# Head pairs of the value product side by side, wider transposes of maxima, another bank for denominators and another band entry, in a two-layer encoder

## The chip, the cores and the metric

The kernel runs on one core of a Trainium2 chip. The metric is the device time of one execution in microseconds (us). Five engines work beside each other, each through its own queue of instructions in a fixed order: TensorE (PE; its loads of stationary operands are listed apart, as PEld), VectorE (DVE), ScalarE (ACT), GpSimd (POOL) and SyncE (SP), which starts the DMA transfers. PE writes its results into PSUM, which has eight banks of 128 partitions x 512 float32; the other engines read them from there.

## The reference

An encoder trunk of two layers over 1024 tokens of width 1024, float32 throughout. Each layer adds a mixer and then a SwiGLU feed-forward part to the stream, each behind an RMS norm:

```python
for layer in range(DEPTH):                      # DEPTH = 2
    u = rms_norm(h, g_mix[layer])
    if layer % 2 == 0:
        h = h + mla_stick_breaking_mixer(u, ...)   # 8 + 8 heads of 64
    else:
        h = h + chunk_band_mixer(u, ...)           # 16 heads of 64
    u = rms_norm(h, g_ffn[layer])
    h = h + swiglu(u, w_gate[layer], w_up[layer], w_down[layer])
return rms_norm(h, g_final)
```

The mixer of the first layer has eight heads of latent attention (MLA: queries and keys through low-rank projections, a rotary part, a softmax under a block-causal mask) and eight heads of stick-breaking attention (strictly causal, no softmax). That of the second layer is a band attention: each chunk of 64 tokens sees itself and the eight chunks ahead of it, with a learned bias by clipped relative distance, and a softmax. What the change touches is the end of each attention: `p @ v` for every head, the softmax's denominators (the sum of the exponentials), and the row maxima that are taken off ahead of the exponential.

## The kernel before, in words

**Tiles.** Everything is held transposed, features on partitions and tokens along the free axis, in tiles of 128 x 512; the 1024 tokens are two halves of 512 (`hf` 0 and 1). A product in full precision is three passes over split operands (`mm3`, lines 286 to 291: high x high, low x high, high x low); the value product, the denominators and the transposes of maxima take plain float32, for which the trace shows two records per instruction.

**Stages,** by the trace: the norm and the stick-breaking heads from 0 to 400 us, MLA with the output projection to 640, the first feed-forward part to 1326, the band's entry to 1384, six band pairs of heads to 1726 (57 us each), the last two and the output projection to 1840, the second feed-forward part to the end.

**Attention.** Heads go in pairs, one of them on partitions 0 to 63 and the other on 64 to 127. For a pair and a half of the queries, `soft_step` goes over the key tiles `j` of 128 keys: scores for both heads into a two-bank tile "z", exponentials on ACT into a tile "a" (2 x 512), their running sum on POOL ("b", line 1085; DVE in the last pairs), and, some steps later, `weighted`, the value product. It adds, for each head `e`, 64 x 128 values times 128 keys x up to 512 queries into half of the partitions of one output bank "o": two instructions, for e = 0 and e = 1, that write columns `cs` of the partitions `rh`. Later key tiles have fewer columns (512, 384, 256, 128). When the last tile is in, `soft_finish` sums the exponentials over the keys with a product with ones, again one instruction per head (line 1101) into the first bank of a "z" tile; ACT makes the reciprocal from Ln and Exp (lines 1103, 1104), DVE improves it with one Newton step (1105, 1106) and multiplies the output with it (1107).

**Maxima.** Ahead of a pair's half, all its scores are computed once for their row maxima: `mla_max` (line 1062, maxima on DVE in line 1064), `band_max` (line 1188, maxima on DVE in line 1191). `neg_max_rows` collects the maxima in one of two 128 x 2 x 32 tiles `maxes` (line 1044), turns 36 columns of it with a product with the identity into a "z" tile (line 1046), and DVE multiplies rows 0 to 3 and 32 to 35 into the queries as additional rows (line 1048), which the score products (lines 1133 to 1135 in MLA, 1214 and 1215 in the band) then read.

**PSUM.** Three kinds of tile share the eight banks: "mm" (two of one bank, for projections), "z" (two of two banks, for scores, maxima, denominators) and "o" (two of one bank, for outputs and statistics of the norms). A tile is handed out again when its last reader is done.

**What sets the order.** In the mixers the code only gives the dependences and an order of writing, with the attention's steps and the projections of the next pair woven together (`weave`); a list scheduler with a cost model then sets the order on each engine. In the feed-forward parts instructions stay in the order of the program.

**Band entry.** `to_mixer1` takes each finished tile of the first feed-forward part, and with the last tile of a half `close` computes the statistics of the norm (line 322 on PE, line 352 for those by column). `mixer1` then computes the values of the first two head pairs for both halves (`vgen(0, [0, 1])`), the first pair's queries and keys (`band_project`; for this pair DVE casts the weights' high parts) and its maxima.

## Time and profile before

| what | value |
|---|---|
| median of 3 runs | 2552.98 us (2551.01 to 2554.29) |
| profiled execution | 2553.58 us |
| its span in the trace | 2551.9 us |
| mean granted clock of PE | 0.995 |
| chain that ended last, by engine | PE 74%, DVE 8%, DMA 1%, ACT 1% |

The busy time of an engine is given for the whole span and for stretches of it; a stretch in which PE is nearly always busy is shortened only by less work for PE or by closing the gaps that are there. In a timeline, the start of an instruction and the start of the next one on the same engine say more than its duration, since products overlap: full-width three-pass products of 512 columns follow each other every 0.23 us, though each lasts 0.39. "x4" are four records of the same form that follow each other directly. Behind an instruction stands in brackets for how long its engine had been idle, and what ended that.

### The profile page before, as it was taken

To read this page: it belongs to the slowest core of one execution; us is meant where nothing else is said; L and a number is where in the kernel's file an instruction comes from. 1 tells how busy PE (TensorE), PEld (TensorE's weight loads), DVE (VectorE), ACT (ScalarE), POOL (GpSimd) and SP (SyncE) were. 2 spreads that over 40 slices of the span, in tenths; PEclk is the share of its full clock that TensorE was granted. 3 is DMA by queue.
4 is the path that set the end of the run, shared out by engine and by line. 5 is a ranking of instruction groups with operands and counts; after the bars stand their busy time and mean duration, and the time that the engine had idled before them with its cause. 6 is when DMAs were issued, how large, how long until landed. Compare 5 with 4: busy or idle time off the path is not lost.

```text
span 2551.9 us, 33625 instructions
## 1 busy us (share of the span) xinstructions
PE 2478.1 (97%) x11710; PEld 1938.4 (76%) x11710; DVE 1858.1 (73%) x3072; ACT 1152.1 (45%) x1996; POOL 493.8 (19%) x475
## 2 busy tenths in 40 slices
PE   9999989999999999999999999999999999999997
PEld 7776766557778888888888777776777888888886
DVE  7988796565886666677766777777788676667775
ACT  5777565344454434433353443334445443443324
POOL 0333335652000000000031334345200000000004
PEclk9999999999999999999999999999999999999998
DMA  5222102125434334476652222223633433447661
GB/s 155 54 65 64 41 26 60 54 84 165 153 124 149 120 128 145 149 259 211 227 167 69 79 87 75 75 93 98 190 128 128 148 130 118 145 156 261 217 208 71
DMA packets 182250, 323.91 MB, mean 127 GB/s; under 512 B 21312, under 2 KB 37568, under 8 KB 182080
## 3 DMA queue, kind: packets, MB, share of 16 engines
q1 hardware_dynamic: 182080, 321.76, 38.0%
q8 instruction: 93, 1.52, 0.2%
q14 instruction: 77, 0.63, 0.1%
HBM read 222.58 MB, written 84.41 MB: 120 GB/s over the span
## 4 chain that ended last, share of the span: by engine, by line
PE 74%; DVE 8%; DMA 1%; ACT 1%; issue 1%; POOL 0%; DVEq 0%; SPq 0%; ACTq 0%; POOLq 0%
PE z L76 25%; PE mm L76 13%; PE o L76 7%; PE mm L289 6%; PE mm L290 6%; PE mm L291 6%; PE o L844 4%; DVE u L76 2%; PE z L1214 1%; PE z L1188 1%; PE z L1215 1%; PE z L1133 1%; DVE u L312 1%; PE z L1101 1%; PE z L1134 1%
## 5 line engine op out<-in xcount | busy, mean ns | idle before, releaser
L76 PE MATMUL z<-u,wh 128*128 128x512 f32 x976 | 302.3, 390 | 6.5 <-DVE u L76 6.5
L76 PE MATMUL z<-u,vh 128*128 128x512 f32 x976 | 301.8, 390 | 2.8 <-DVE u L76 2.8
L289 PE MATMUL mm<-u,wh 128*128 128x512 f32 x720 | 287.8, 400 | 3.5 <-DVE f L1003 1.4
L290 PE MATMUL mm<-u,wh 128*128 128x512 f32 x720 | 283.8, 394 | 0.0
L291 PE MATMUL mm<-u,wl 128*128 128x512 f32 x720 | 282.4, 393 | 0.0
L257 POOL TENSOR_TENSOR wl<-wr,wh 128x512 fp32r<-128x512 f32 (+2 forms) x95 | 122.0, 1289 | 803.3 <-ACT wh L252 736.0
L76 PE MATMUL mm<-u,wh 128*128 128x512 f32 x720 | 223.4, 392 | 4.6 <-ACT wh L76 4.6
L76 PEld LDWEIGHTS z<-u,wh 128*128 128x128 f32 x976 | 183.2, 188 | 47.5 <-DVE u L76 9.5
L76 PEld LDWEIGHTS z<-u,vh 128*128 128x128 f32 x976 | 182.9, 188 | 43.1 <-ACT u L76 4.4
L76 PE MATMUL z<-u,wl 128*128 128x512 f32 x488 | 190.0, 389 | 1.4 <-DVE wl L76 1.4
L76 PE MATMUL z<-u,vl 128*128 128x512 f32 x488 | 189.9, 389 | 0.0
L289 PEld LDWEIGHTS mm<-u,wh 128*128 128x128 f32 x720 | 135.4, 188 | 54.7 <-issue 27.6
L76 PEld LDWEIGHTS mm<-u,wh 128*128 128x128 f32 x720 | 134.7, 188 | 35.6 <-ACT wh L76 6.9
L290 PEld LDWEIGHTS mm<-u,wh 128*128 128x128 f32 x720 | 135.5, 188 | 27.2 <-issue 3.2
L291 PEld LDWEIGHTS mm<-u,wl 128*128 128x128 f32 x720 | 135.3, 188 | 27.3 <-issue 0.9
L844 PE MATMUL o<-a,u 128*64 128x512 f32 (+3 forms) x768 | 154.6, 474 | 0.0
L76 PE MATMUL mm<-u,vh 128*128 128x512 f32 x496 | 152.7, 389 | 0.0
L76 PE MATMUL mm<-u,wl 128*128 128x512 f32 x360 | 140.8, 391 | 0.8 <-DVE wl L76 0.5
L257 POOL TENSOR_TENSOR u<-wr,u 128x512 fp32r<-128x512 f32 x8 | 10.9, 1374 | 669.5 <-ACT u L252 669.5
L1085 POOL TENSOR_TENSOR b<-b,a 128x512 f32<-128x512 f32 (+3 forms) x80 | 110.1, 1377 | 125.8 <-ACT a L1217 104.1
L1216 DVE TENSOR_TENSOR a<-z,bias 128x1024 f32<-128x1024 f32 (+3 forms) x96 | 78.2, 823 | 76.9 <-PE z L1215 71.0
L76 ACT CAST vh<-vr 128x512 fp32r<-128x512 f32 (+1 forms) x166 | 96.1, 579 | 82.5 <-DVE vr L76 31.5
(244 smaller groups left out, 5859.4 us busy)
## 6 DMA issues: line engine op xcount, KB each, us to landing
u<-f_t SPq DMA_DIRECT2D x144, 256.0 KB, 5.0
vr<-in_w_up SPq DMA_DIRECT2D x88, 256.0 KB, 4.4
wr<-in_w_gate SPq DMA_DIRECT2D x88, 256.0 KB, 3.7
f_t<-x SPq DMA_DIRECT2D x72, 256.0 KB, 2.0
wr<-in_w_out SPq DMA_DIRECT2D x64, 256.0 KB, 3.1
f_t<-e SPq DMA_DIRECT2D x54, 256.0 KB, 3.6
ld<-f SPq DMA_DIRECT2D x54, 256.0 KB, 5.1
u<-u SPq DMA_DIRECT2D x96, 128.0 KB, 2.2
```

What stands on the lines that cost most here:

```text
L76: return lambda *a, **k: self.tc.keep_in_program_order(f(*a, **k))
L257: self.eng(eng).tensor_tensor(lo, src, hi.bitcast(F32), ALU.subtract)
L289: mm(out, wh, xh, start=first, stop=False, skip_group_check=onto)
L290: mm(out, wh, xl, start=False, stop=False, skip_group_check=onto)
L291: mm(out, wl, xh, start=False, stop=last, skip_group_check=onto)
L312: self.eng(eng).tensor_tensor(acc, acc, sq, ALU.add)
L844: self.nc.tensor.matmul(o[rh, cs], vt[j // 4][:, j % 4, rh], w[:, e, cs], start=first, stop=last)
L1085: self.eng("dve" if dest[2] else "pool").tensor_tensor(st["esum"][:, :, cs], old[:, :, cs], ex[:, :, cs], ALU.add)
L1101: nc.tensor.matmul(den[64 * e:64 * e + 64, :], self.ones[:, 0:64], esum[:, e, :], start=True, stop=True)
L1133: mm(z[:, e, cs], kth[0:kr, bs], qh[0:kr, cs], start=True, stop=False)
L1134: mm(z[:, e, cs], kth[0:96, bs], ql[0:96, cs], start=False, stop=False)
L1216: nc.vector.tensor_tensor(ex[:, :, cs], z[:, :, cs], tk[:, :, xs], ALU.add)
```

## The change

There are four parts. First, `weighted` writes head 1's instruction with the highest priority and with the condition that it is issued right behind head 0's (`joined`, which keeps the last such instruction in `self.joint`); the two instructions of a denominator are tied in the same way. Second, `maxes` has 2 x 64 columns instead of 2 x 32, all 128 columns are turned, and the rows read are 0 to 3 and 64 to 67. Third, the denominators go into an "o" bank. Fourth, the band's entry runs in another order: values of half 0, then the closing of half 1 (moved there from the end of the feed-forward part), the first pair's projection, and then the values of half 1, for which the value weights are loaded and split a second time; the first pair's high parts are cast by ACT instead of DVE.

```diff
@@ -29,6 +29,7 @@
 LOADS = 4
 AHEAD = 2
 LAG = 2
+TOP = 100000
 
 TOGETHER = 4
 G_MIX0, G_FFN0, G_MIX1, G_FFN1, G_FIN, G_CQ, G_CKV, G_N = 0, 8, 16, 24, 32, 40, 43, 45
@@ -228,7 +229,7 @@
         self.tri, self.carry_ones = self.masks[:, 0:P], self.masks[:, P:2 * P]
         self.zeros = self.masks[:, 2 * P:3 * P]
 
-        self.maxes = [cp.tile([P, 2, 32], F32, name=f"maxes{i}") for i in range(2)]
+        self.maxes = [cp.tile([P, 2, 64], F32, name=f"maxes{i}") for i in range(2)]
         for m in self.maxes:
             nc.vector.memset(m, 0.0)
         self.negblk = small[0:4, 16:20]
@@ -837,11 +838,22 @@
                 v, q = vts[g][hf][:, r, :], ps[:, (b - b0) * ncol + g * P:][:, :P]
                 self.nc.scalar.activation(v, q, AF.Identity, scale=s.rc[hf][:, r:r + 1])
 
-    def weighted(self, o, vt, j, w, cs, first, last):
-
-        for e in range(2):
+    def joined(self, make, *args):
+
+        with self.tc.high_priority(offset=TOP), self.tc.issue_after(self.joint.ins):
+            self.joint = make(*args)
+
+    def weighted(self, o, vt, j, w, cs, first, last, join=False):
+
+        def head(e):
             rh = slice(64 * e, 64 * e + 64)
-            self.nc.tensor.matmul(o[rh, cs], vt[j // 4][:, j % 4, rh], w[:, e, cs], start=first, stop=last)
+            return self.nc.tensor.matmul(o[rh, cs], vt[j // 4][:, j % 4, rh], w[:, e, cs], start=first, stop=last)
+
+        if join:
+            self.joined(head, 0)
+        else:
+            self.joint = head(0)
+        self.joined(head, 1)
 
 
 
@@ -1043,10 +1055,10 @@
         m = self.maxes[0]
         nc.vector.reduce_max(m[:, :, 0:4], m2[:, :, :, :nh], axis=AX.X)
         mt = self.banks()
-        nc.tensor.matmul(mt[0:36, 0, 0:P], m.rearrange("p a b -> p (a b)")[:, 0:36], self.ident, start=True, stop=True)
+        nc.tensor.matmul(mt[:, 0, 0:P], m.rearrange("p a b -> p (a b)"), self.ident, start=True, stop=True)
         for e in range(2):
             nc.vector.tensor_tensor(dsts[e].rearrange("p (a b) -> p a b", a=4),
-                                    mt[32 * e:32 * e + 4, 0, None, 0:P].to_broadcast([4, 4, P]),
+                                    mt[64 * e:64 * e + 4, 0, None, 0:P].to_broadcast([4, 4, P]),
                                     self.negblk[:, :, None].to_broadcast([4, 4, P]), ALU.mult)
 
     def mla_max(self, hf, proj):
@@ -1096,9 +1108,13 @@
 
     def soft_finish(self, o, esum, row, k, keep):
         nc = self.nc
-        den = self.banks()[:, 0, :]
-        for e in range(2):
-            nc.tensor.matmul(den[64 * e:64 * e + 64, :], self.ones[:, 0:64], esum[:, e, :], start=True, stop=True)
+        den = self.out_bank()
+
+        def total(e):
+            return nc.tensor.matmul(den[64 * e:64 * e + 64, :], self.ones[:, 0:64], esum[:, e, :], start=True, stop=True)
+
+        self.joint = total(0)
+        self.joined(total, 1)
         r, ot = self.tmp("f"), self.tmp("f")
         nc.scalar.activation(r, den, AF.Ln)
         nc.scalar.activation(r, r, AF.Exp, scale=-1.0)
@@ -1144,7 +1160,7 @@
 
         nc, a = self.nc, self.a
         for i in range(2):
-            w = self.weight(a["w_qk1"][2 * p + i], eng_hi="dve", eng_lo="dve" if p == 0 else "pool")
+            w = self.weight(a["w_qk1"][2 * p + i], eng_hi="act" if p == 0 else "dve", eng_lo="dve" if p == 0 else "pool")
             for hf in hfs:
                 ps = self.bank()
                 yield from self.dense(ps, w, s.u[hf], range(KD))
@@ -1316,10 +1332,12 @@
             vts = [[] for _ in range(8)]
             vgen = lambda g, hf: self.values([a["w_v1"][2 * g], a["w_v1"][2 * g + 1]], u, 4, KD, 1,
                                              vts[2 * g:2 * g + 2], hf)
-            self.now(vgen(0, [0, 1]))
+            self.now(vgen(0, [0]))
+            self.close(u, 1, columns=True)
             new = lambda: ([[], []], [[], []])
             proj = new()
             self.now(self.band_project(0, u, proj))
+            self.now(vgen(0, [1]))
             tq, tk = self.band_bias(0, "bias_q"), self.band_bias(0, "bias_k")
             self.now(self.band_max(0, proj, tq))
             for p in range(8):
@@ -1363,7 +1381,7 @@
             h = s.h[hf][m]
             self.feed(nxt, hf, h, G_MIX1 + m)
             nc.sync.dma_start(h1_d[hf][m], h)
-            if m == KD - 1:
+            if m == KD - 1 and hf == 0:
                 self.close(nxt, hf, columns=True)
 
         with self.phase("ffn0", FFN_TEMPS):
```

By engine, PE keeps its number of instructions, DVE keeps its own (four subtractions more and four casts less), ACT has 8 more, SP has 4 more (transfers of 256 KB). The order on PE is the same up to the middle of the first MLA pair, and in the feed-forward parts. Three places show what moves. A row gives the line, the operation, output<-inputs and the output's shape; a number behind a name tells buffers apart, and "x2" is both heads, one behind the other. Lines 844, 1046, 1062, 1101 and 1133 to 1135 are lines 850, 1058, 1074, 1114 and 1149 to 1151 after the change, and 289 to 291 are 290 to 292.

PE before, in the first MLA pair (o816: its output bank, z: scores, a: exponentials of one key tile, u: values, queries and keys):

```order
L844 MATMUL o816_4094<-a799_4014,u698_3592 64x512
L1133 MATMUL z818_4098<-u658_3450,u733_3777 128x512
L1134 MATMUL z818_4098<-u659_3451,u733_3777 128x512
L1135 MATMUL z818_4098<-u658_3450,u734_3778 128x512
L1133 MATMUL z818_4098<-u685_3552,u736_3785 128x512
L1134 MATMUL z818_4098<-u686_3553,u736_3785 128x512
L1135 MATMUL z818_4098<-u685_3552,u737_3786 128x512
L1062 MATMUL z820_4108<-u754_3846,u785_3961 128x128
L1062 MATMUL z820_4108<-u757_3854,u805_4047 128x128
L844 MATMUL o816_4094<-a799_4014,u698_3592 64x512
L844 MATMUL o816_4094<-a802_4033,u698_3592 64x512
L1133 MATMUL z822_4115<-u658_3450,u733_3777 128x384
```

PE after, at the same place:

```order
L1149 MATMUL z818_4098<-u658_3450,u733_3777 128x512
L1150 MATMUL z818_4098<-u659_3451,u733_3777 128x512
L1151 MATMUL z818_4098<-u658_3450,u734_3778 128x512
L1149 MATMUL z818_4098<-u685_3552,u736_3785 128x512
L1150 MATMUL z818_4098<-u686_3553,u736_3785 128x512
L1151 MATMUL z818_4098<-u685_3552,u737_3786 128x512
L1074 MATMUL z820_4108<-u754_3846,u785_3961 128x128
L1074 MATMUL z820_4108<-u757_3854,u805_4047 128x128
L850 MATMUL o816_4094<-a799_4014,u698_3592 64x512 x2
L1149 MATMUL z822_4115<-u658_3450,u733_3777 128x384
L1150 MATMUL z822_4115<-u659_3451,u733_3777 128x384
```

Before, head 1 of tile a799 stands eight instructions behind its head 0 and beside head 0 of tile a802; after, both heads of a799 stand together, and a802 follows later.

PE before, in a later MLA pair, from the last scores for the maxima (z954) to the transpose (z955) and the first scores that need it (z958; mm: a projection):

```order
L1062 MATMUL z954_4665<-u852_4243,u882_4366 128x512
L1062 MATMUL z954_4665<-u855_4251,u903_4458 128x512
L289 MATMUL mm1002_4865<-u681_3538,wh1000_4861 128x512
L290 MATMUL mm1002_4865<-u682_3539,wh1000_4861 128x512
L291 MATMUL mm1002_4865<-u681_3538,wl1001_4862 128x512
L1046 MATMUL z955_4673<-ident_153,maxes0_161 36x128
L1133 MATMUL z958_4681<-u882_4366,u840_4198 128x512
```

PE after, from the same scores on:

```order
L1074 MATMUL z954_4665<-u852_4243,u882_4366 128x512
L1074 MATMUL z954_4665<-u855_4251,u903_4458 128x512
L290 MATMUL mm965_4704<-u596_3176,wh963_4700 128x512
L291 MATMUL mm965_4704<-u597_3177,wh963_4700 128x512
L850 MATMUL o956_4677<-a920_4536,u700_3596 64x512 x2
L292 MATMUL mm965_4704<-u596_3176,wl964_4701 128x512
L850 MATMUL o956_4677<-a929_4569,u700_3596 64x384 x2
L290 MATMUL mm965_4704<-u601_3198,wh963_4700 128x512
L291 MATMUL mm965_4704<-u602_3199,wh963_4700 128x512
L292 MATMUL mm965_4704<-u601_3198,wl964_4701 128x512
L850 MATMUL o956_4677<-a944_4620,u700_3596 64x256 x2
L850 MATMUL o956_4677<-a951_4651,u700_3596 64x128 x2
```

and then:

```order
L1114 MATMUL o974_4750<-b931_4578,ones_151 64x512 x2
L1058 MATMUL z955_4673<-ident_153,maxes0_161 128x128
L290 MATMUL mm1002_4865<-u674_3516,wh1000_4861 128x512
L291 MATMUL mm1002_4865<-u675_3517,wh1000_4861 128x512
L292 MATMUL mm1002_4865<-u674_3516,wl1001_4862 128x512
L1149 MATMUL z958_4681<-u882_4366,u840_4198 128x512
```

Before, one triple of a projection stands between the scores z954 and the transpose; after, two triples' worth of projections, four value products of o956 and the denominator o974, and one triple stands between the transpose and z958.

PE before, at a denominator of another MLA pair (z1031) and the first value product of the next half (o1048):

```order
L291 MATMUL mm1030_4957<-u625_3304,wl1029_4954 128x512
L1101 MATMUL z1031_4963<-b968_4722,ones_151 64x512 x2
L1133 MATMUL z1035_4975<-u960_4693,u934_4589 128x128
L1134 MATMUL z1035_4975<-u961_4694,u934_4589 128x128
L1135 MATMUL z1035_4975<-u960_4693,u935_4590 128x128
L1133 MATMUL z1035_4975<-u972_4743,u937_4597 128x128
L1134 MATMUL z1035_4975<-u973_4744,u937_4597 128x128
L1135 MATMUL z1035_4975<-u972_4743,u938_4598 128x128
L844 MATMUL o1048_5011<-a994_4844,u701_3598 64x512 x2
```

PE after, at the same denominator, which is now in an output bank (o1031):

```order
L1114 MATMUL o1031_4963<-b968_4722,ones_151 64x512 x2
L1149 MATMUL z1035_4975<-u960_4693,u934_4589 128x128
L1150 MATMUL z1035_4975<-u961_4694,u934_4589 128x128
L1151 MATMUL z1035_4975<-u960_4693,u935_4590 128x128
L1149 MATMUL z1035_4975<-u972_4743,u937_4597 128x128
L1150 MATMUL z1035_4975<-u973_4744,u937_4597 128x128
L1151 MATMUL z1035_4975<-u972_4743,u938_4598 128x128
L290 MATMUL mm1030_4957<-u625_3304,wh1028_4953 128x512
L291 MATMUL mm1030_4957<-u626_3305,wh1028_4953 128x512
L292 MATMUL mm1030_4957<-u625_3304,wl1029_4954 128x512
L290 MATMUL mm1030_4957<-u630_3326,wh1028_4953 128x512
```

and then:

```order
L291 MATMUL mm1030_4957<-u631_3327,wh1028_4953 128x512
L292 MATMUL mm1030_4957<-u630_3326,wl1029_4954 128x512
L1074 MATMUL z1058_5047<-u934_4589,u1025_4946 128x512
L850 MATMUL o1048_5011<-a994_4844,u701_3598 64x512 x2
L850 MATMUL o1048_5011<-a1013_4900,u701_3598 64x384 x2
```

Before, the six scores stand between the two; after, two triples of a projection and one instruction of the maxima's scores more, and the denominator and o1048 take turns in the output banks.

## Rows read from the trace of the kernel before

**Rows 1.** The page, part 1: busy us, share of the span, instructions, by engine

```profile
PE 2478.1 (97%) x11710; PEld 1938.4 (76%) x11710; DVE 1858.1 (73%) x3072; ACT 1152.1 (45%) x1996; POOL 493.8 (19%) x475
```

**Rows 2.** Stretches: us, then PE, PEld, DVE, ACT, POOL busy (instructions), granted clock, DMA

```profile
400.00:640.00 240.00, 232.62 (x1021) 148.72 (x1021) 146.79 (x194) 99.46 (x156) 125.25 (x91) 0.99 0.32 97
...
1326.00:1384.00 58.00, 58.00 (x349) 50.90 (x348) 28.42 (x56) 16.48 (x35) 7.13 (x8) 1.00 0.20 61
1384.00:1726.00 342.00, 333.60 (x1934) 259.40 (x1935) 253.81 (x558) 140.27 (x246) 135.51 (x134) 1.00 0.26 82
```

**Rows 3.** Timeline of PE, a pair alone: start us, us, instruction, count, [idle before]

```profile
198.12 0.39 PE L291 MATMUL mm<-u,wl 128*128 128x512 f32 x1
198.44 1.08 PE L844 MATMUL o<-a,u 128*64 128x512 f32 x4
199.45 0.50 PE L289 MATMUL mm<-u,wh 128*128 128x512 f32 x1
199.79 0.39 PE L290 MATMUL mm<-u,wh 128*128 128x512 f32 x1
```

**Rows 4.** The same, one head alone

```profile
421.98 1.07 PE L844 MATMUL o<-a,u 128*64 128x512 f32 x2
422.98 0.50 PE L289 MATMUL mm<-u,wh 128*128 128x512 f32 x1
```

**Rows 5.** The same, a pair and one head more

```profile
440.65 1.93 PE L844 MATMUL o<-a,u 128*64 128x512 f32 x6
442.51 0.50 PE L1133 MATMUL z<-u,u 104*128 104x512 f32 x1
```

**Rows 6.** One line's instructions, lines 844 and 1046: count, ns, first and last start, forms

```profile
L844 PE MATMUL o<-a,u x768: 272/486/644, 72.0 to 1836.1; 128*64 128x512 f32 x72, 128*64 128x256 f32 x41, 128*64 128x384 f32 x40, 128*64 128x128 f32 x39
L1046 PE MATMUL z<-ident,maxes x48: 271/272/300, 411.7 to 1796.3; 128*36 128x128 f32 x48
```

**Rows 7.** Timeline of PE around a transpose of maxima with 36 columns

```profile
1455.69 0.39 PE L290 MATMUL mm<-u,wh 128*128 128x512 f32 x1
1456.01 0.41 PE L1046 MATMUL z<-ident,maxes 128*36 128x128 f32 x2
...
1456.69 0.39 PE L291 MATMUL mm<-u,wl 128*128 128x512 f32 x1
```

**Rows 8.** The same around a full-width product in plain float32, two passes

```profile
347.81 1.02 PE L322 MATMUL o<-u,ones 128*128 128x512 f32 x2
...
348.90 0.40 PE L290 MATMUL mm<-u,wh 128*128 128x512 f32 x1
```

**Rows 9.** Waits of PE, 400 to 640 us: us in total, times, longest

```profile
PE z L1046 <- DVE maxes L1044: 3.8, 2, 2.0
PE z L1133 <- DVE u L1048: 1.0, 1, 1.0
```

**Rows 10.** Timeline of PE around the longest of these waits

```profile
521.70 0.62 PE L1062 MATMUL z<-u,u 104*128 104x512 f32 x2
...
525.05 0.38 PE L1046 MATMUL z<-ident,maxes 128*36 128x128 f32 x2 [2.04 <-DVE maxes L1044]
```

**Rows 11.** Windows after it, columns as in the stretches

```profile
528.00:530.00 2.00, 2.00 (x6) 1.52 (x6) 0.50 (x1) 1.92 (x3) 1.28 (x1) 0.50 0.31 83
530.00:532.00 2.00, 2.00 (x8) 1.62 (x7) 0.69 (x1) 1.03 (x3) 0.00 (x0) 0.76 0.02 8
```

**Rows 12.** Timeline of all engines, a typical denominator, lines 1101 to 1106

```profile
438.03 1.08 PE L1101 MATMUL z<-b,ones 128*64 128x512 f32 x4
...
441.19 0.69 DVE L1106 SCALAR_TENSOR_TENSOR f<-z,f 128x512 f32<-128x512 f32 x1
```

**Rows 13.** Timelines of PE and DVE, the slowest denominator

```profile
1746.63 1.08 PE L1101 MATMUL z<-b,ones 128*64 128x512 f32 x4
...
1753.24 0.68 DVE L1106 SCALAR_TENSOR_TENSOR f<-z,f 128x512 f32<-128x512 f32 x1
```

**Rows 14.** Waits of PE, 1384 to 1726 us

```profile
PE z L1214 <- DVE a L1216: 7.3, 6, 1.2
```

## The prediction

> **What bounds the kernel now.** I read the shares of the span by engine first. TensorE (PE) is busy for 2478.1 of 2551.9 us, 97%; VectorE (DVE) follows with 1858.1, 73% [rows 1]. So the span is a sum of PE instructions with few gaps, and two things can shorten it: PE work that becomes cheaper, and gaps that close. Next I read the busy time stage by stage [rows 2]. In the attention of the first layer (400 to 640 us) PE is busy for 232.62 of 240 us, in the band pairs (1384 to 1726) for 333.60 of 342, and at the band's entry (1326 to 1384) for all 58.00. DVE has 146.79 of 240 and 253.81 of 342: room, but in the band not much. Then the gaps: in the first layer's attention the largest are waits for the row maxima and for what is made of them [rows 9], in the band six equal ones of 1.2 us behind the scores' bias add [rows 14]. The profiled execution took 2553.58 us, 0.60 above the median of 2552.98, so a sum made against it is lowered by 0.6 at the end.
>
> **Part 1, the second head's product behind the first's.** One head's product is two float32 passes that use half of the array's columns. What a pass costs follows from three places in the timeline. Two heads side by side, 512 columns each, start at 198.44 and the next instruction at 199.45: 1.01 us for four passes [rows 3]. One head alone goes from 421.98 to 422.98: 1.00 us for two passes [rows 4]. So the second head beside the first costs nothing. A pair and one head more, also 512 wide, take 440.65 to 442.51, 1.86 us [rows 5]. The head that has no neighbour costs 0.85 us. What is left of the 1.01 is a price per run of such products, 0.16, and the full-width instructions at both edges add to it: the first start comes 0.32 after its predecessor and the second neighbour follows 0.34 after the first, where the pace of such instructions is 0.23 [rows 3]. That is 0.09 and 0.11 more, about 0.35 us per run.
>
> There are 768 records of the product, so 192 pairs of heads with two passes each [rows 6]. I counted both orders of PE. Before, 161 of the 192 have head 1 directly behind head 0; in 31 it stands later, as in the first excerpt of the change. Some of these already share the array with a different tile's head, so I count columns and not pairs: for every run, the longer of its two halves. That sum goes from 87,168 to 79,872 columns and the number of runs from 136 to 116. Columns: 7296 / 512 x 0.85 = 12.1 us less. Runs: 20 x 0.35 = 7.0 us less. Together -19.1. By stage: stick-breaking -1.2, attention of the first layer -12.2, band -5.7. Nothing hides this on PE, which has the work on the path; what could hide it is another engine that comes late, taken up below.
>
> The Trainium skill, "TensorE: Matmul & The Clock Gate", Part 3 (Packing small matmuls), says that a weight load overlaps running products only where it goes to other rows of the array. The two heads share all 128 rows. By that rule a pair would pay for the second load, and the column part of the gain would be smaller or nothing. The trace speaks against it: 1.01 us for the pair and 1.00 for the single.
>
> **Part 2, transposes with 128 columns.** From 1455.69 to 1456.69 lie line 290, the transpose, and one 512-column line 1214 [rows 7]; less 2 x 0.23 the transpose costs 0.54 us. A full-width product in plain float32, two passes of 512 columns, takes from 347.81 to 348.90 with one 512-column product between, 1.09 - 0.23 = 0.86 us [rows 8], so by its columns 128 wide ones cost 0.86 / 4 = 0.22. No row shows a transpose of that form. Bounds: it stays at 0.54 (nothing gained), or it costs 0.22 (0.32 gained). I take 0.24, near the second end, since line 322 shows no edge cost with its 128 columns and the edge is the larger part of the 0.54. Of 24 transposes [rows 6], 21 stand alone before, away from other half-width runs: 21 x 0.30 = -6.3, of that -1.5 in the first layer and -4.8 in the band. The two reads on DVE only start at another partition, and their size is unchanged.
>
> **A gap that closes.** At 525.05 PE waits 2.04 us for the maxima [rows 10], because the last scores for them, line 1062 at 521.70, stand only 0.7 us of products ahead of the transpose in the order. Line 1133 then waits 0.96 for DVE's two reads [rows 9]. Right behind, the granted clock is 0.50 and then 0.76 [rows 11]: the lower of its two levels, 1.2 of 2.4 GHz, for one whole window and about half of the next, after PE had stood still for 3.0 us in two pieces. At half speed 2.0 us lose 1.0, and 0.76 in 2 us loses 0.48. In the new order (second excerpt) some 5.4 us of PE work stand between the scores and the transpose, and one triple of products between the transpose and its reader; 0.4 of the second wait stays. 2.04 + 0.56 + 1.5 = -4.1.
>
> **Part 3, denominators in an output bank.** The denominator now takes one of two "o" banks, and the next segment's first product needs that bank back, after line 1106 has read it. Typically that is 441.19 + 0.69 - 438.03 = 3.85 us after the denominator's start [rows 12], at worst 1753.24 + 0.68 - 1746.63 = 7.29 [rows 13]. Queued behind the product that waits are all later PE instructions. By the new order the PE work between the two is 4.7 to 6.3 us at most places of the first layer, 3.3 at one (third excerpt), 6.5 to 7.4 in the last two band pairs, and 12 or more in the other pairs. At the short place 0.5 is lost. Bounds for all nine close places: 0, or 6 if each is as slow as half-way between typical and worst. I take +0.8. The score banks that come free let the band's maxima products (line 1188) come sooner, and then DVE's reading of them is what they wait for; nothing in the trace prices that, bounds 0 to 1.2 per pair (the wait already there, [rows 14]), I take 0.3 x 7 = +2. The denominator may stand nearer to the last add on GpSimd: +1 (0 to 2). The new orders of transposes elsewhere: +0.5. Together +4.3.
>
> **Part 4, the band's entry.** Half 0's values come first, then half 1's statistics are closed, then projection, then half 1's values. PE has no gap there to fill [rows 2], so nothing is won unless a gap is made: 0 (-1 to +1). The weights of the values are now fetched and cast twice: four transfers of 256 KB, four casts on ScalarE and four subtractions on DVE. ScalarE is busy there for 16.48 and DVE for 28.42 of 58 us [rows 2], so both have room, and the transfers run while PE has 58 us of other products; without that cover a late half of values would stop PE for the length of its casts.
>
> **Sum.** -19.1 - 6.3 - 4.1 + 4.3 = -25.2. A faster PE meets the other engines earlier; I take a tenth of what the first layer's attention gains in parts 1 and 2, 13.7, as new small waits: +1.4. That makes -23.8: 2553.6 - 23.8 = 2529.8 against the profiled execution, 2529.2 against the median, rounded to 2529.
>
> **The rivals.** (a) *Half or all of the gain in the first layer is swallowed.* There PE already waits for DVE's maxima [rows 9], and their reductions are fed by PE itself; against it, DVE has 93 us free in 240 [rows 2]. All 13.7 lost gives 2543, half 2536. (b) *Pairs stand together but don't run together,* since the second head's load holds the first up: 12.1 lost, 2541; rows 3 and 4 speak against it. (c) *More gain:* the six waits at line 1214 go, too, since score banks come free sooner: 7.3 more [rows 14], 2522. Against it: their order on PE, DVE and ScalarE is as before, and they wait for DVE's add, not for a bank. (d) *Slower: the output bank is held too long.* If at the nine close places DVE comes to line 1106 as late as in [rows 13], the next product waits 7.3 - 4 = 3.3, and a fall of the clock as in [rows 11] follows for 1.5: 9 x 4.8 = +43 on -28.1 (the sum without part 3 and its +4.3), about 2568. It decides from 28.1 / 9 = 3.1 us per place. Against it: typical 3.85 us stand against 4.7 or more of work.
>
> **How the numbers follow.** About 0.2%, 5 us, is what a measurement of this kernel can tell from no change. Forecast, 2523 to 2536: 0.62. (a) and (b), 2536 to 2548: 0.18, of that 0.02 for (b). (c) or another gain, below 2523: 0.10. New waits that eat all but 5 us, in several places: 0.06. (d): 0.04. Faster is 0.62 + 0.18 + 0.10 = 0.90, the same 0.06, slower 0.04. The range 2520 to 2543 leaves out some 0.05 of (a), 0.04 of (c) and the last two cases, a little under 0.2.
>
> **What would show it.** Every record of the product comes in fours or more, with 1.0 us for a pair of 512 that stands alone; the transposes of maxima take some 0.25 from their neighbours; the stretch of the first layer's attention is 15 to 18 us shorter, the band's pairs some 7 to 10; PE's waits for maxima in the first layer fall under 2 us in sum, and waits of line 844 for line 1106 stay under 2. It is wrong if PE's idle time in these stretches grows by more than 5 us, if the first layer keeps its length, or if the transpose keeps its 0.54.

## The result, and the profile after

The changed kernel takes 2536.18 us (median of 4 runs, 2535.75 to 2541.07), the kernel before 2553.64 (4 runs): ratio 0.9934, interval 0.9918 to 0.9950, or 17.5 us less. The prediction was 2529, range 2520 to 2543, faster with 0.90; its forecast case ended at 2536. The sign and the range hold, and more than a quarter of the forecast gain is missing. The profiled execution of the changed kernel took 2536.20, its span is 2534.4.

The same landmark in both traces gives the time by stage. The landmarks are the first product of a norm's statistics (line 322, 323 after; 28.91 us before, 27.98 after), the first product of the first feed-forward part (635.70 us before, 621.58 after), the first denominator of the band (1406.31, 1393.20), that of the sixth band pair (1692.70, 1679.13), the first product of the second feed-forward part (1842.70, 1826.26) and the last product (2542.3, 2525.1):

| stretch | predicted, its terms sorted by place | measured |
|---|---|---|
| start to the first product of the statistics | 0 | -0.9 |
| from there to the end of the first layer's mixer | -16.6 | -13.2 |
| first feed-forward part and band entry, to the first band denominator | -0.6 | +1.0 |
| the five band pairs from there | -1.5 | -0.5 |
| the rest of the band and the output projection | -5.1 | -2.9 |
| second feed-forward part | 0 | -0.7 |
| sum | -23.8 | -17.2 |

The 0.9 us at the start is none of the change's: PE has the same order in both kernels there, and in the fourteen traces of this document the landmark lies anywhere from 27.98 to 29.91. The second feed-forward part, too, has the same order in all of them and takes 695.3 to 702.1 us. So single stretches are compared where something changes, and a microsecond in the total is not read as the work of a part.

PE's busy time fell as the span did, and its share stayed at 97%, against [rows 1]. The page of the changed kernel, part 1:

```profile
PE 2460.9 (97%) x11710; PEld 1934.4 (76%) x11710; DVE 1870.9 (74%) x3072; ACT 1155.3 (46%) x2004; POOL 493.7 (19%) x475
```

Every head now has its neighbour. In the timeline of PE after (line 850 is 844 before), a pair alone:

```profile
447.27 1.08 PE L850 MATMUL o<-a,u 128*64 128x512 f32 x4
448.28 0.50 PE L290 MATMUL mm<-u,wh 128*128 128x512 f32 x1
```

1.01 us for a pair, as in [rows 3]. Summed over all runs of half-width products, from their first start to the next instruction's, with what the full-width neighbours lose at the edges and without idle time, it is 195.9 us before and 177.6 after: -18.3, where the prediction had -19.1. By stage: -12.7 to the end of the first layer's mixer, 0 at the entry and in the five pairs, -5.6 in the rest of the band.

The transposes of maxima after, one in the first layer and one in the band, from the timeline of PE:

```profile
449.08 0.40 PE L290 MATMUL mm<-u,wh 128*128 128x512 f32 x1
449.32 0.38 PE L1058 MATMUL z<-ident,maxes 128*128 128x128 f32 x2
449.45 0.48 PE L291 MATMUL mm<-u,wh 128*128 128x512 f32 x1
449.77 0.39 PE L292 MATMUL mm<-u,wl 128*128 128x512 f32 x1
...
1441.71 0.39 PE L291 MATMUL mm<-u,wh 128*128 128x512 f32 x1
1442.05 0.49 PE L1058 MATMUL z<-ident,maxes 128*128 128x128 f32 x2
1442.29 0.48 PE L1230 MATMUL z<-u,u 128*128 128x512 f32 x1
1442.61 0.39 PE L292 MATMUL mm<-u,wl 128*128 128x512 f32 x1
```

In the first layer it takes 449.77 - 449.08 - 2 x 0.23 = 0.23 us, where a narrow one took 0.54 (in [rows 7], and at 454.21 us in the first layer, too); the prediction had 0.24. In the band it takes 1442.61 - 1441.71 - 2 x 0.23 = 0.44: it starts 0.34 after its predecessor instead of 0.23, because the maxima are ready only just then.

The gap of [rows 10] is closed. The transpose at that place and its neighbours after, from the timeline of PE:

```profile
510.54 1.03 PE L1114 MATMUL o<-b,ones 128*64 128x512 f32 x4
511.50 0.49 PE L1058 MATMUL z<-ident,maxes 128*128 128x128 f32 x2
...
512.78 0.48 PE L1149 MATMUL z<-u,u 100*128 100x512 f32 x1
```

No idle time stands in brackets, neither at the transpose nor at its reader, line 1149 (1133 before); the 0.4 that the prediction left there is gone as well, and so is the fall of the clock behind it. But other gaps are there. PE's waits after, from 400 to 640 us, then from 1384 to 1720 and from 1720 to 1830; columns as in [rows 9]:

```profile
PE z L1149 <- ACT a L1152: 1.7, 1, 1.7
PE z L1058 <- DVE maxes L1056: 1.7, 1, 1.7
PE mm L291 <- DVE u L258: 1.2, 1, 1.2
PE o L850 <- DVE f L1122: 0.4, 1, 0.4
...
PE z L1230 <- DVE a L1232: 7.3, 6, 1.2
...
PE z L1204 <- DVE m L1207: 1.2, 2, 1.0
PE z L1058 <- DVE maxes L1056: 0.7, 2, 0.5
```

The six waits of [rows 14] are as they were, now at line 1230. Of the denominators' bank (line 1122 is 1106 before) one wait of 0.4 is left, where the prediction had 0.8. The clock falls to its lower level (0.50, 1.2 of 2.4 GHz) at two new places. Windows after, columns as in [rows 2], the granted clock is the third number from the end:

```profile
408.00:410.00 2.00, 1.63 (x6) 1.24 (x7) 1.91 (x4) 1.24 (x2) 1.29 (x2) 0.84 0.45 125
410.00:412.00 2.00, 2.00 (x7) 1.54 (x6) 1.59 (x3) 0.62 (x1) 1.56 (x2) 0.50 0.68 165
412.00:414.00 2.00, 2.00 (x9) 1.60 (x8) 0.76 (x1) 1.37 (x2) 0.92 (x1) 0.80 0.57 138
568.00:570.00 2.00, 0.51 (x2) 0.45 (x3) 0.69 (x1) 2.00 (x3) 1.27 (x1) 0.95 0.45 113
570.00:572.00 2.00, 2.00 (x7) 1.52 (x6) 1.23 (x1) 0.35 (x1) 0.00 (x0) 0.50 0.65 215
572.00:574.00 2.00, 2.00 (x8) 1.60 (x7) 0.73 (x1) 1.02 (x1) 0.00 (x0) 0.70 0.09 33
```

The first costs 2 x (0.16 + 0.50 + 0.20) = 1.7 us, the second 2 x (0.05 + 0.50 + 0.30) = 1.7. The first stands behind PE's wait of 1.72 for the first maxima, which the kernel before had too, without a fall; the second behind the wait for line 1152.

### The profile page after: what moved, and what is told of

It is laid out like the page before. It is cut to its first block, busy times and chain, and to the rows that moved or that the text cites. A ratio compares the mean times of both kernels' runs of the same rounds, so it can differ in the third digit from the quotient of the medians.

```text
span 2534.4 us, 33597 instructions
## 1 busy us (share of the span) xinstructions
PE 2460.9 (97%) x11710; PEld 1934.4 (76%) x11710; DVE 1870.9 (74%) x3072; ACT 1155.3 (46%) x2004; POOL 493.7 (19%) x475
## 4 chain that ended last, share of the span: by engine, by line
PE 71%; DVE 9%; DMA 2%; ACT 2%; issue 1%; POOL 1%; DVEq 0%; POOLq 0%; SPq 0%; ACTq 0%
PE z L77 25%; PE mm L77 12%; PE o L77 7%; PE mm L290 6%; PE mm L291 5%; PE mm L292 5%; PE o L850 3%; DVE u L77 2%; PE z L1230 1%; PE z L1231 1%; PE z L1204 1%; DVE u L313 1%; PE z L1149 1%; PE o L1114 1%; PE z L1074 1%
## 5 line engine op out<-in xcount | busy, mean ns | idle before, releaser
L850 PE MATMUL o<-a,u 128*64 128x512 f32 (+3 forms) x768 | 139.2, 474 | 0.5 <-DVE f L1122 0.4
L1233 ACT ACTIVATE a<-a 128x1024 f32<-128x1024 f32 (+3 forms) x96 | 70.0, 737 | 129.7 <-DVE a L1232 128.8
```

The lines of the kernel that those rows point to most:

```text
L850: return self.nc.tensor.matmul(o[rh, cs], vt[j // 4][:, j % 4, rh], w[:, e, cs], start=first, stop=last)
L1233: nc.scalar.activation(ex[:, :, cs], ex[:, :, cs], AF.Exp)
```

## The experiments

Theory: the gain is the columns and runs that the tie saves on PE; the wide transposes and the band's entry add nothing, because what follows them waits for VectorE; what is missing to the forecast went into falls of the clock and into VectorE's chain. Rivals: all four parts add up at their price on PE; or the denominators' bank carries the gain. Each part alone and each part undone, then combinations. All medians are of 4 to 10 runs, and a ratio is against the kernel before on the same chip (2553.6 to 2554.5). The three groups below ran on different chips, so a difference between two changed kernels of different groups is weaker evidence than the ratios. A stage's change is read at the landmarks above and against the trace of the kernel before, the first layer's mixer from the first product of the statistics on.

### Each part alone

The tie alone:

```diff
+        if join:
+            self.joined(head, 0)
+        else:
+            self.joint = head(0)
+        self.joined(head, 1)
```

> The kernel before with the second head's value product tied behind the first's, and nothing else. By the order of PE all 192 pairs stand together (161 before), the longer halves of the runs sum to 79,872 columns (87,168) and there are 121 runs (136). First theory, the tie carries nearly all of the change's gain of 17.5 us: columns 7296/512 x 0.85 = 12.1 and runs 15 x 0.35 = 5.3 less, 2.5 us of it lost again in new waits, so 15 us faster (13 to 17). Rival, the tie needs the denominators in another bank to pay: 8 us faster or less, with PE waiting for denominators' banks.

Measured: 2543.78, ratio 0.9962 (0.9947 to 0.9977), 10.7 us faster; neither the first theory's 13 to 17 nor the rival's 8. The half-width products fell by 17.7 us in the trace, as counted. Part of that went into a second fall of the clock between 400 us and the end of the first layer's mixer (1.7 us) and into 2.1 us more of PE's waits for maxima in the last band pairs: the first layer's mixer gained 9.5, the end of the band 2.0. The gap at the transpose (2.10 and 0.96 us of idle PE) stays in this order, so its closing is no work of the tie alone.

The wide transposes alone (the tile and the rows read go with them, as in the change):

```diff
-        nc.tensor.matmul(mt[0:36, 0, 0:P], m.rearrange("p a b -> p (a b)")[:, 0:36], self.ident, start=True, stop=True)
+        nc.tensor.matmul(mt[:, 0, 0:P], m.rearrange("p a b -> p (a b)"), self.ident, start=True, stop=True)
```

> The kernel before with 128-column transposes of maxima, and nothing else; the order on PE is the same. First theory, in the band what follows the transpose waits for VectorE anyway, so only the five transposes in the first layer pay 0.3 us each, and those of the band pay next to nothing: 1 to 3 us faster. Rival, the price of 0.3 us is paid back at all 21 places: 6.3 us faster.

Measured: 2554.23, ratio 1.0002 (0.9993 to 1.0012): no change, less than either. In the trace the transposes did cost less where they stand between full-width products: ten of them in the five band pairs took 3.9 us instead of 5.6 without idle time, and three in the first layer 0.23 each instead of 0.54. The five pairs became 0.3 shorter. In the first layer the gain was lost at the three transposes that stand in runs of half-width products, which the prediction had put at nothing. One of them, from the timeline of PE, before and with the wide form:

```profile
501.41 0.87 PE L844 MATMUL o<-a,u 128*64 128x384 f32 x4
502.11 0.38 PE L1046 MATMUL z<-ident,maxes 128*36 128x128 f32 x2
502.42 0.50 PE L289 MATMUL mm<-u,wh 128*128 128x512 f32 x1
```

```profile
502.11 0.86 PE L844 MATMUL o<-a,u 128*64 128x384 f32 x2
502.90 0.49 PE L1046 MATMUL z<-ident,maxes 128*128 128x128 f32 x2
503.32 0.86 PE L844 MATMUL o<-a,u 128*64 128x384 f32 x2
504.11 0.50 PE L289 MATMUL mm<-u,wh 128*128 128x512 f32 x1
```

The wide form stands between the two heads and they run one behind the other: 2.00 us for the three instructions instead of 1.01. A second place lost 0.78 in the same way, and a third 0.71, of which 0.56 took the place of idle time. A new fall of the clock at 412 us took 1.7 on top.

The denominators in an output bank alone:

```diff
-        den = self.banks()[:, 0, :]
+        den = self.out_bank()
```

> The kernel before with the denominators in an output bank, untied, and nothing else. The order moves with it: 179 pairs of heads stand together instead of 161, 124 runs instead of 136, 85,760 columns instead of 87,168. First theory, only these counts matter: 1408/512 x 0.85 = 2.3 and 12 x 0.35 = 4.2, so 6.5 us faster, less some 2 of new waits: 4 to 6. Rival, value products wait for the denominator's bank: no faster than before, or slower.

Measured: 2545.44, ratio 0.9967 (0.9955 to 0.9978), 9 us faster, more than the counts alone. In this order the gap of [rows 10] is closed: no fall of the clock from 400 us to the end of the first layer's mixer, and 8.7 us gained there. In the band a fall of the clock at 1580 us took 1.7 back.

The band's entry alone (and, as in the change, the closing of half 1 taken out of the feed-forward part and the first pair's casts on ACT):

```diff
-            self.now(vgen(0, [0, 1]))
+            self.now(vgen(0, [0]))
+            self.close(u, 1, columns=True)
...
+            self.now(vgen(0, [1]))
```

> The kernel before with the band entered in the other order, and nothing else. PE had no gap there to fill. First theory, it makes a small gap of its own, since the products for the maxima now come behind one another faster than VectorE reads them: 0.5 to 1.5 us slower. Rival, no change within 0.5 us; a gain of more than 0.5 us would say that the gap at the end of the feed-forward part is what it closes.

Measured: 2553.97, ratio 1.0000 (0.9990 to 1.0009). No change by the medians, whose interval of about 2.4 us either way holds the rival and the theory alike. The traces put the cost at 0.5 us, as shown at the old entry below.

### Each part undone

The changed kernel without the ties, with narrow transposes, with the denominators in a score bank, and with the old entry (only the lines that name the part are shown):

```diff
-        self.joint = total(0)
-        self.joined(total, 1)
+        for e in range(2):
+            nc.tensor.matmul(den[64 * e:64 * e + 64, :], self.ones[:, 0:64], esum[:, e, :], start=True, stop=True)
```

(and `weighted` as in the kernel before)

> The changed kernel without the ties (value products and denominators untied); the other three parts stay. 179 pairs together, 124 runs, 85,760 columns, as with the denominators alone moved. First theory, the parts add up: 9 to 11 us slower than the changed kernel (5888/512 x 0.85 = 9.8 and 8 runs x 0.35 = 2.8 more, less the waits that the faster order has made), near 2546. Rival, the other parts carry the gain: within 4 us of the changed kernel, 2540 or less.

Measured: 2545.39, ratio 0.9968 (0.9955 to 0.9981). 9.2 us slower than the changed kernel, as the first theory says: the tie is worth 9 to 12 us alone (10.7), beside the rest (9.2) and beside the output bank (11.8, by the combination below).

```diff
-        nc.tensor.matmul(mt[:, 0, 0:P], m.rearrange("p a b -> p (a b)"), self.ident, start=True, stop=True)
+        nc.tensor.matmul(mt[0:36, 0, 0:P], m.rearrange("p a b -> p (a b)")[:, 0:36], self.ident, start=True, stop=True)
```

> The changed kernel with 36 columns in the transposes of maxima again; the order on PE is that of the changed kernel. First theory, only the transposes that stand among products without a wait lose: 1.5 to 3 us slower, 2538 to 2539. Rival, each of the 20 loses 0.3: 6 us slower, 2542.

Measured: 2534.62, ratio 0.9921 (0.9906 to 0.9936). Not slower but 1.6 faster, against both; the intervals of the two ratios overlap, so this is no proof of a gain. The profiled executions are 5.9 us apart, of which 3.4 stand in the first layer, where this one has no fall of the clock after 400 us and the changed kernel's has two, and 3.2 in the second feed-forward part, where the two kernels are the same.

```diff
-        den = self.out_bank()
+        den = self.banks()[:, 0, :]
```

> The changed kernel with the denominators in a score bank again, still tied in pairs. 192 pairs together, 79,872 columns, 121 runs instead of 116. First theory, 5 x 0.35 = 1.8 us slower, 2538. Rival, the output bank costs as much in waits as the fewer runs give: the same within 1 us, or faster.

Measured: 2539.71, ratio 0.9946 (0.9931 to 0.9961), 3.5 slower; the theory had 1.8. The output bank is no burden. What the theory left out: the gap of [rows 10] is back in the trace (2.1 and 0.9 us). It stands in all five traces of kernels with the denominators in a score bank (before, tie alone, wide alone, entry alone, and this one) and in none of the nine others.

```diff
-            self.now(vgen(0, [0]))
-            self.close(u, 1, columns=True)
+            self.now(vgen(0, [0, 1]))
...
-            self.now(vgen(0, [1]))
```

> The changed kernel with the band entered in the old order. First theory, the new waits of 1.1 us at the maxima's products of the entry go away: 0.5 to 1.5 us faster, 2535. Rival, they come back at the first band pair, since VectorE's chain there is the same: within 0.5 us.

Measured: 2532.59, ratio 0.9915 (0.9899 to 0.9932), 3.6 faster; more than the theory's 1.5. The two profiled executions are only 0.8 us apart, and they differ most where the order is the same: the first layer's mixer ends 2.3 us earlier, because the wait of 1.74 at 569 us and the fall behind it are missing. The timelines of ACT and PE show why, first of the changed kernel, then of this one:

```profile
567.38 0.62 ACT L253 CAST u<-ld 128x512 fp32r<-128x512 f32 x1 [3.96 <-DMA ld<-o]
568.42 1.02 ACT L1152 ACTIVATE a<-z 128x1024 f32<-128x1024 f32 x1
569.49 0.55 PE L1149 MATMUL z<-u,u 100*128 100x512 f32 x1 [1.74 <-ACT a L1152]
```

```profile
566.61 0.62 ACT L253 CAST u<-ld 128x512 fp32r<-128x512 f32 x1 [2.29 <-DMA ld<-o]
567.66 1.01 ACT L1152 ACTIVATE a<-z 128x1024 f32<-128x1024 f32 x1
568.73 0.50 PE L1149 MATMUL z<-u,u 100*128 100x512 f32 x1
```

A cast that waits for a transfer stands ahead of the exponential on ACT. Seen from the transpose ahead of it (563.27 and 564.17), the tile came 4.1 us later in the one execution and 2.4 in the other, from the same program up to there. Of the nine kernels with the output bank only one other, the one with priority for the maxima, has a wait there in its trace (1.53), so this looks like a matter of the execution; how often the changed kernel meets it is not known, and with it most of the 3.6 us stays unexplained. The entry itself costs what the traces show between the band's first product of values and its first denominator: 80.28 us before, 80.70 to 80.84 in the five kernels with the new entry, 80.17 to 80.28 in the eight others, the combinations below among them. That is 0.5 us, and PE's waits at the maxima's products there (line 1204) show it: 1.0 to 1.1 us in the five, 0.4 to 0.5 in the others.

### Combinations

The two parts that gain, tie and output bank, without the other two:

> The kernel before with the ties and the denominators in an output bank; transposes with 36 columns and the old band entry. First theory, these two parts carry the whole gain, the band's entry costs 1.0 us and the wide transposes nothing: 2531 to 2534, 20 to 23 us faster than before. Rival, the wide transposes give 1.5 us in the first layer: 2534 to 2536.

Measured: 2533.60, ratio 0.9922 (0.9905 to 0.9940), 20.0 us faster; just inside the first theory. Two of the four parts do all that the change does; the 2.5 us more are not clear of the intervals.

What is left in the band is the wait of 1.2 us in each pair. The chain up to it, from the timeline of all engines of the changed kernel:

```profile
1458.31 0.63 ACT L1233 ACTIVATE a<-a 128x512 f32<-128x512 f32 x1 [1.80 <-DVE a L1232]
1458.96 0.62 ACT L253 CAST u<-t 64x512 fp32r<-64x512 f32 x1
...
1459.08 1.29 POOL L1097 TENSOR_TENSOR b<-b,a 128x512 f32<-128x512 f32 x1 [2.80 <-PE z L1204]
1459.61 1.30 DVE L258 TENSOR_TENSOR u<-t,u 64x512 fp32r<-64x512 f32 x1 [1.34 <-ACT u L253]
1460.95 0.43 DVE L1232 TENSOR_TENSOR a<-z,bias 128x256 f32<-128x256 f32 x1
1461.43 0.44 PE L1230 MATMUL z<-u,u 128*128 128x384 f32 x1 [1.21 <-DVE a L1232]
```

PE needs the score bank that DVE's add (line 1232) reads; the add stands behind a subtraction (258) that waits for ACT's cast (253), and the cast stands behind an exponential (1233) whose own add came late, since that one, too, stood behind two subtractions. The experiment gives the add priority on DVE:

```diff
-                nc.vector.tensor_tensor(ex[:, :, cs], z[:, :, cs], tk[:, :, xs], ALU.add)
+                with self.tc.high_priority(offset=50):
+                    nc.vector.tensor_tensor(ex[:, :, cs], z[:, :, cs], tk[:, :, xs], ALU.add)
```

> The last one (ties and output bank), and in the band the add of the bias to the scores has priority over what else VectorE has ready, so that it stands ahead of the two subtractions behind a cast of ScalarE. First theory, the wait of 1.2 us in each of the first six band pairs is VectorE's queue held by a subtraction that waits for ScalarE's cast; it goes, and the six pairs take 56.0 us instead of 57.2: 7 us faster than the last one. Rival, the subtraction that comes later now holds up the maxima or the next projection: 2 us faster or less, with another wait in its place in each pair.

Measured: 2526.86, ratio 0.9892 (0.9873 to 0.9910): 6.7 faster than the two parts alone and 26.7 faster than the kernel before, the fastest of all. The same place, with the waits of PE from 1360 to 1840 us below it:

```profile
1455.23 0.62 ACT L253 CAST u<-t 64x512 fp32r<-64x512 f32 x1 [1.22 <-PE z L1230]
1455.88 0.69 DVE L258 TENSOR_TENSOR u<-t,u 64x512 fp32r<-64x512 f32 x1 [1.09 <-ACT u L253]
1456.60 0.42 DVE L1233 TENSOR_TENSOR a<-z,bias 128x256 f32<-128x256 f32 x1
1457.08 0.44 PE L1230 MATMUL z<-u,u 128*128 128x384 f32 x1 [0.20 <-DVE a L1233]
...
PE z L1230 <- DVE a L1233: 1.2, 6, 0.2
```

The same subtraction still stands ahead of this add, but the cast is no longer late, because the exponential ahead of it has been done. And the subtraction itself is shorter: from its start to PE's product it is 1.82 us above and 1.20 here, since it took 1.30 beside GpSimd's add (line 1097) and takes 0.69 now that GpSimd's add is just over, which starts after the exponential and so earlier, too. That is 0.6 of the 1.0 us; the earlier start is the rest. Six waits of 0.2 stay of six of 1.2, and the five pairs became 5.1 us shorter than in the two-part kernel (280.95 after 286.04). The theory holds in what the edit does, with the shorter subtraction as a part that it did not have. The prediction's case (c), which gave these waits a small chance to go, named the wrong way out, as its own objection says: what counts is the add's place in DVE's queue, and not the banks that the denominators leave.

Priority for the whole block of the maxima as well (reduction, transpose and reads), and then the wide transposes on top:

```diff
+        with self.tc.high_priority(offset=50):
+            m = self.maxes[0]
...
```

> The last one, and the reduction of the maxima, its transpose and VectorE's reads of it have priority, too. In the band the order stays, in the first layer a transpose's maxima stand three VectorE instructions earlier at one place. First theory, PE's waits for maxima in the first layer shrink a little: 0 to 1.5 us faster than the last one. Rival, no change within 0.5 us.

> The last one with 128-column transposes; the order is the same. In the band the wide form cut the transposes' own time by 1.7 us in ten of them without the stage becoming shorter. First theory, it was the wait of 1.2 us in each pair that took the gain back, so without that wait the band and the first layer gain 2.5 to 4 us together. Rival, VectorE's reads of the maxima right behind the transpose take it back: within 1.5 us of the last one, and the band's stage the same.

Measured: 2528.81, ratio 0.9901 (0.9880 to 0.9922), and 2529.49, ratio 0.9904 (0.9884 to 0.9923). Neither can be told from 2526.86. With the wide form ten transposes cost 4.5 instead of 5.7 us, and their stretch is 281.0 instead of 281.2. So the first theory for the wide form falls: it wasn't the wait of 1.2 us that took its gain. What does, the timelines of DVE, PE and its loads show, before and after:

```profile
1455.67 0.17 DVE L1044 TENSOR_REDUCE maxes<-m 128x8 f32<-128x16 f32 x1
1456.47 1.40 DVE L1048 TENSOR_TENSOR u<-z,scalars 4x512 fp32r<-4x512 f32 x2
...
1457.20 0.19 PEld L1215 LDWEIGHTS z<-u,y 68*128 68x128 f32 x1
```

```profile
1441.82 0.17 DVE L1056 TENSOR_REDUCE maxes<-m 128x8 f32<-128x16 f32 x1
1442.62 1.40 DVE L1060 TENSOR_TENSOR u<-z,scalars 4x512 fp32r<-4x512 f32 x2
...
1443.07 0.40 PE L291 MATMUL mm<-u,wh 128*128 128x512 f32 x1
1443.36 0.19 PEld L1231 LDWEIGHTS z<-u,y 68*128 68x128 f32 x1 [0.33 <-DVE u L1060]
...
1443.70 0.40 PE L1230 MATMUL z<-u,u 128*128 128x512 f32 x1
```

From the reduction to DVE's read of the turned maxima it is 0.80 us either way. The load for the first product that needs them, line 1231 (1215 before), had not waited for that read before and now waits 0.33, and from 1443.07 to 1443.70 PE takes 0.63 us for two products instead of 0.46. So it saves 0.1 at the transpose and loses 0.17 a few products later. Three pairs of kernels differ in nothing but the form, with the same order on PE: from the band's first product to the second feed-forward part the wide form is 0.4 us shorter alone, 0.1 longer in the changed kernel and 0.4 shorter here.

## Why the prediction was right, point by point, and where it was short

- **Part 1, the columns and runs (-19.1):** right, -18.3 by the trace, and by stage as forecast. Case (b) is out: with every pair adjacent, one of 512 columns takes 1.01 us, and the second head costs nothing. The rule behind that case, that loads overlap only where they go to other rows (the Trainium skill, "TensorE: Matmul & The Clock Gate", Part 3, Packing small matmuls), disagrees with this trace, and the measurement decides.
- **Part 2, the transposes (-6.3):** the price was right where PE sets the pace and both neighbours are of full width, 0.23 us in the first layer. The step that failed is the count: 21 places were taken at full price, and the 16 in the band hardly pay, since the maxima are ready only at the start of the transpose, and the read behind it is what the next product needs. That is -4.8 in the sum against -0.4 to +0.1 measured in the band, the largest miss. The three places beside half-width products were put at nothing, and there the wide form costs more; with the ties it parts no two heads, and one such place is left, between two tiles, with a loss of 0.4. The kernel with this part alone shows no gain at all.
- **The gap that closes (-4.1):** right, with its fall of the clock. The kernels show what closes it: the order that comes with the denominators' new bank. The gap is gone in all nine kernels that have it and stands in all five that don't.
- **Part 3, waits for the output bank (+0.8 in +4.3):** right in kind, 0.4 at one place, and case (d), slower by these waits, was far off. Waits of line 1204 (1188 before) came to 1.2 in the last pairs, of +2, and none in the five pairs; but the kernel with the ties and no output bank has 1.4 there, so the banks that come free are not shown to be their cause. No wait of PE for the last add on GpSimd shows (+1 in the sum).
- **Part 4, the entry (0, -1 to +1):** in its bounds, +0.5, by waits at the maxima's products.
- **A tenth for new waits (+1.4):** the waits themselves were fewer than forecast. PE's idle time in both mixers grew by 0.7 us, where the gap, part 3 and this term together had -2.6 + 4.3 + 1.4 = +3.1. In the first layer it even fell, by 1.9, although two waits are new there (1.7 for a transfer that came late, and 1.2 for a subtraction, which all nine kernels with the output bank have). What the term lacked is the clock: two falls of 1.7 us each are new, one is gone. The sum had the fall that goes and none that comes.

So the size failed by the 16 transposes in the band (some 4.5 us) and by the clock (+1.7, where -1.5 was in the sum); the tie gave what was counted. Part of these misses is hidden by what came out better by no merit of the forecast: fewer waits (2.4 us), and a start and feed-forward parts that were 1.1 us shorter in this execution. About 1.0 us in the first layer's attention I can't place. Two of the signs that the prediction named did not come: its first layer's stretch should have become 15 to 18 us shorter and the band's pairs 7 to 10, and they became 13.2 (14.1 with the start) and 3.4.

## What to carry to other kernels

Count saved work on the busiest engine place by place, and at each ask when the instruction's input and its reader's input are ready: a cheaper instruction between two waits for another engine gave next to nothing here, and one that parts two instructions that run side by side cost up to 1.0 us. A short wait that returns in every round is best followed through the queues of all engines to the one instruction that stands in front for no reason; moving that one gave 6.7 us, a third of what two parts had given on PE. Take the parts of a bundled change apart: two of four gave all of the gain.

## What the runs showed of the hardware

- The same wait doesn't always bring the clock down. PE waits 1.72 or 1.73 us for the first maxima at 408 to 412 us in all fourteen traces; behind it the granted clock falls to 0.50 (1.2 of 2.4 GHz) in nine and stays in five (the kernel before, the denominators alone, the entry alone, narrow transposes, the add first). A fall costs 1.7 us, so medians of this kernel 2 us apart say little about a change that makes or removes no more than that, and stretches say more than totals. What decides it isn't shown here.
- A subtraction of 64 x 512 on DVE took 1.30 us instead of 0.69 while GpSimd ran an add of 1.29 that had started 0.5 earlier; with the add just over it took 0.69 (at 1459.61 and 1455.88 above). It counts which of the two starts first. In the trace of the changed kernel, from the band on, the subtractions that start while an add or a subtraction on GpSimd has 0.16 to 0.90 us left take 0.71 to 1.44 us, which is 0.55 more than what is left; those that start ahead of GpSimd's instruction keep 0.68 or 0.69 (in the trace before even with 0.61 us side by side), as do the 46 that run beside none.
- A transpose of 128 columns took 0.44 us from PE in the band and 0.23 in the first layer. In the band its records last 0.49 against 0.41 with 36 columns [rows 7], so the result came no sooner, though the next instruction did.
- A transpose of 36 columns shares a run of half-width products, and one of 128 parts it: two heads of 384 columns and the transpose took 1.01 us with 36 and 2.00 with 128 (at 501.41 and 502.11 above).
